# A convolution moved into PSUM by halves of 512 tokens, with three banks each for the up and down products

## The chip, the cores and the metric

The kernel runs on one core of one Trainium2 chip. The metric is the device time of one execution in microseconds (us), lower is better. The times are medians of several runs.

A core has five engines that work side by side, each through its own queue in order: TensorE (PE in the profile; PEld is its loading of weights), VectorE (DVE), ScalarE (ACT), GpSimd (POOL) and SyncE (SP, which issues the DMAs here). Tiles lie in SBUF. TensorE writes its results to PSUM, which has eight banks; a bank holds 512 float32 values in each of 128 partitions.

## The reference

Two layers of a decoder for 1024 tokens of 1024 values in float32. Each layer is a mixer (three kinds of attention) with a residual, and then the part that this change is in, a gated MLP with a causal convolution of width 3 over the tokens:

```python
h = rms_norm(x, g_ffn[l])
u = causal_dwconv(h @ w_up[l], conv_w[l], conv_b[l])   # y[t] = b + u[t]*w2 + u[t-1]*w1 + u[t-2]*w0
gate, up = u[..., :D_FF], u[..., D_FF:]                # D_FF = 2816
x = x + (jax.nn.silu(gate) * up) @ w_down[l]
```

## The kernel before

The function `ffn` computes the out-projection and the MLP of one layer. It runs once per layer: in the profiled execution the MLP's products stand from about 718 to 1450 us and from about 2140 to 2867 us.

Channels of the MLP lie on partitions and tokens along the free axis. The loop goes over the 22 blocks of 128 gate channels, each with its block of 128 up channels; the text calls one such pair of blocks a channel block. Four steps belong to each:

- **Up-projection** (`ups`, products on L958). A float32 product is made of three matmuls of operands split into a high and a low part. Two of the 22 channel blocks take eight half products per pair of blocks, the other 20 take seven by sums and differences of half blocks of weights (DVE on L990, L991, L995 and L1009, in place in the raw weights). Each half product needs two split weights `wu` (ACT copies the high part on L198, POOL subtracts it for the low part on L203) and 12 matmuls. The tag `wu` has five slots. The results are gathered in `gu` and `uu` in SBUF: by ACT (L989, L994) and, where sums are formed, by DVE from PSUM (L998, L1001, L1004, L1007, L1011).
- **Convolution** (`conv`, L1014). ACT writes `w2 * u + b` (L1016), and DVE adds the two shifted products in place with two SCALAR_TENSOR_TENSOR instructions (L1019). It is done for the gate (`yg`) and for the up part (`yu`); all of it lies in SBUF.
- **Gate** (`channels`, L1031). ACT applies Silu to `yg` in place (L1037) and DVE multiplies (L1039). All this covers 1024 tokens at once, but for the last channel block, which goes by halves of 512.
- **Down-projection** (`down7`, products on L1059). Two channel blocks together, again by seven products instead of eight: DVE and POOL form sums (L1045), ACT and POOL split (L198, L203), PE multiplies into a bank of PSUM, and DVE adds the bank to `x` (L1063). For one of the products PE goes on accumulating in a bank after DVE has read it out (`start=False` on L1089). The last two channel blocks use `down` (L1115, L1118) instead.

PSUM banks are handed out in rings by `bank(use)`. In this phase the ring `a` of the out-projection and the down products has four banks and the ring `u` of the up products has four (`B3`, L67). For the last down products `a` is set to `B4`.

The order of the instructions on each engine is settled when the program is built: a scheduler places them by its own estimate of durations, with priorities at some places, and each engine then runs its queue in that order. An instruction that has to wait holds up everything behind it on its engine.

Of the kernel before, what the change touches and what calls it, by code (L numbers as in the profile page):

```python
# [14 lines left out]
AF = mybir.ActivationFunctionType  # L15
# [3 lines left out]
S = 1024  # L19
# [9 lines left out]
# Engines of the splits into hi and lo: of the in-projection's chunks and of the rest.  # L29
# [6 lines left out]
# SBUF of each phase: runs of a start in kB and tags (name, number, kB).  # L36
# [23 lines left out]
# PSUM banks of each phase, by use.  # L60
# [6 lines left out]
B3 = {'a': (3, 6, 0, 7), 't': 'a', 'u': (4, 5, 1, 2)}  # L67
# Priorities and paces.
# [11 lines left out]
# Blocks of tokens between the down-projection and what follows it, by layer.  # L80
LAG = (2, 1)
# Channels of the up-projection that go without the seven products, and the order of these.
# [3 lines left out]
# Query heads of each chunk of the in-projection.  # L86
QH = (6, 2, 0, 0, 4, 0)
# Blocks of rows whose selection ScalarE counts.
# [8 lines left out]
class View:  # L97
    """The tiles of one phase at fixed places: each tag a ring of slots, each slot a pool of its own. Slots below cut are stacked from the left, the others from the right."""

    def __init__(self, tc, cut, top, *runs):  # L100
        """Each run is a start in kB and tags (name, number, kB) that follow one another from it."""
# [9 lines left out]
        def slot(o, side, kb):  # L111
            """A pool of one slot, which reaches kb kB, to its neighbour."""
            pool = tc.tile_pool(name=f"at{int(o * 256)}", bufs=1, side=side, reuse_waits="tile")
            self.pools[o] = self.ctx[side].enter_context(pool), int(kb * 256)
# [24 lines left out]
class Trunk:  # L139
# [19 lines left out]
    def banks(self, **uses):  # L159
        """The PSUM banks of a phase, by use."""  # L160
# [22 lines left out]
    def rstd(self, ss, n, dims):  # L183
        """(ss / dims + eps) ** -0.5 for n columns, dims per column."""
# [9 lines left out]
    def split(self, hi, lo, src, he, le):  # L194
        """src = hi + lo, each of twelve significant bits."""
# [9 lines left out]
    def rope(self, z, t, heads, width, off, half, tabs, pool, eng="vector"):  # L205
        """Rotates z[:, h, off:off + 2 * half] in place; z is [128, heads, width]."""
# [46 lines left out]
    def load_split_in(self, l, segs, pool, engines, slot):  # L253
        """The columns segs of w_in[l], split: four tiles [128, 2, 2, w], hi and lo of two rows of blocks."""
# [16 lines left out]
    def in_proj(self, hT, wc, t, after=None):  # L271
        """One token tile; its matmul M0 waits for the instruction after."""
# [18 lines left out]
    def indexer(self, zi, sc, pool, causal_diag):  # L291
        """Yields between pieces: scores of the indexer, then the selection masks, in place in sc."""
# [52 lines left out]
        # The TOPK-th largest of each row, bit by bit: the largest float that enough values reach.  # L345
        # VectorE counts the values that reach the candidate, in the upper half of the bits on values
        # cut to that half; ScalarE sums signs of differences, so that a value equal to the candidate
        # counts half, which the step after the loop repairs.
# [45 lines left out]
        # need[i]: how many of the values equal to the threshold are still to be taken.  # L394
# [35 lines left out]
    def mla_tile(self, t, ps, kpe, up, pool, outs):  # L430
        """The latents of one token tile to queries, keys and values, stored to DRAM."""
# [44 lines left out]
    def attn_prep(self, H, pool):  # L476
        """Stacked operands of one head: negated scores are the sum of the products of H["ops"]."""
# [7 lines left out]
        else:  # L485
            # [hi | lo] of keys and queries, and the keys as [lo | hi]
# [28 lines left out]
    def attn_prep_v(self, H, pool):  # L515
        """The values of one head as [hi | lo]."""
# [68 lines left out]
    def layer(self, l, hT):  # L585
        nc, tc, a = self.nc, self.tc, self.a
# [23 lines left out]
        # chunk A: indexer and the shared rotary key  # L610
# [227 lines left out]
    def ffn(self, l, mixh, xprev, xspill, hT_next):  # L838
# [96 lines left out]
        for i, j in ((1, 0), (2, 0), (1, 1), (2, 1), (4, 0), (4, 1)):  # L935
            combine(i, j)
# [267 lines left out]
```

## Time and profile before

| | |
|---|---|
| median of 3 runs | 2869.42 us (2868.08 to 2870.92) |
| profiled execution, first to last instruction (its span) | 2867.2 us |
| the median lies above that span by | 2.2 us |
| mean granted clock of TensorE | 0.988 |
| instructions in the profiled execution | 40312 |

| stretch, us | PE busy | DVE busy | ACT busy | POOL busy |
|---|---|---|---|---|
| 718 to 800 (MLP of layer 0 begins) | 71.43 | 65.81 | 33.32 | 57.22 |
| 1400 to 1450 (its end and the next norm) | 45.64 | 43.87 | 21.24 | 16.39 |
| 2140 to 2200 (MLP of layer 1 begins) | 52.02 | 46.66 | 24.65 | 35.72 |
| 2800 to 2867 (its end and the last norm) | 56.17 | 57.14 | 27.84 | 33.99 |

The page gives busy time by engine, the chain that ended last, and the costliest groups of instructions. A group is a line of the kernel, an engine, an operation and its tiles, with the number of instructions, their busy time and mean duration, and the idle time of the engine just before them with what ended it. Matmuls overlap in the pipeline, so PE's busy time is not its work: matmuls of 512 columns that follow one another start every 0.23 us, though each lasts 0.39 us. The view by stretches gives busy time in windows, the timeline gives merged instructions in order of time, and the view of waits tells who waited for whom.

### The profile page before, as it was taken

What the parts mean: (1) busy time and instruction counts of PE and PEld (TensorE: products, weight loads), DVE (VectorE), ACT (ScalarE), POOL (GpSimd) and SP (SyncE); (2) the same over time, 40 slices, a digit from 0 to 9 for tenths busy, and PEclk for the clock granted to TensorE, in tenths of its full rate; (3) what the DMA queues carried; (4) which work ended last, traced back from release to release, by engine and by line L of the source; (5) the groups of instructions that cost most, each with busy time, mean ns of one, the idle gap of its engine ahead of it and who ended that gap; (6) DMA issues with size and microseconds to landing.
All of it is one profiled execution on the core that took longest, in us unless ns stands there. A gap on an engine that the chain in (4) does not pass through costs nothing.

```text
span 2867.2 us, 40312 instructions
## 1 busy us (share of the span) xinstructions
PE 2712.0 (95%) x13576; PEld 2261.2 (79%) x13576; DVE 2353.8 (82%) x4379; ACT 1499.8 (52%) x3160; POOL 1905.0 (66%) x1910
## 2 busy tenths in 40 slices
PE   7999999999899999999999999999998999999998
PEld 7987888878677777777799878988786777777776
DVE  7679997864888888888866899978648888888888
ACT  4565758972444444444445666489624444444444
POOL 4354367961687888878634444679517888888885
PEclk9999999999999999999999999999999999999999
DMA  5322333350111111111333223233500111111112
GB/s 162 104 81 63 98 97 90 97 169 2 37 52 52 45 52 52 59 45 45 95 98 108 78 77 99 79 95 92 164 9 29 53 51 52 52 59 45 45 52 81
DMA packets 224010, 208.82 MB, mean 73 GB/s; under 512 B 21852, under 2 KB 197820, under 8 KB 223804
## 3 DMA queue, kind: packets, MB, share of 16 engines
q1 hardware_dynamic: 223804, 206.26, 23.9%
q8 instruction: 106, 1.74, 0.3%
q14 instruction: 100, 0.82, 0.1%
HBM read 153.80 MB, written 39.85 MB: 68 GB/s over the span
## 4 chain that ended last, share of the span: by engine, by line
PE 23%; POOL 21%; DVE 12%; issue 6%; ACT 3%; DMA 3%; SPq 0%; POOLq 0%; ACTq 0%; DVEq 0%
POOL wu L203 10%; PE psum L284 6%; POOL act L203 4%; POOL wd L203 4%; PE psum L924 3%; PE psum L537 3%; PE psum L958 2%; POOL wr L1045 2%; PE psum L562 2%; DMA wr<-in_w_down_dram 2%; DVE x L1063 2%; DVE yu L1019 1%; PE psum L1059 1%; DVE cut L361 1%; PE psum L1115 1%
## 5 line engine op out<-in xcount | busy, mean ns | idle before, releaser
L203 POOL TENSOR_TENSOR wu<-raw,wu 128x256 fp32r<-128x256 f32 (+1 forms) x584 | 613.2, 1069 | 176.4 <-ACT wu L198 175.2
L284 PE MATMUL psum<-wi,hT 128*128 128x384 f32 (+1 forms) x3072 | 605.7, 340 | 0.2 <-ACT hT L244 0.2
L284 PEld LDWEIGHTS psum<-wi,hT 128*128 128x128 f32 x3072 | 530.5, 190 | 9.8 <-ACT hT L244 0.6
L958 PE MATMUL psum<-hT,wu 128*128 128x512 f32 x1824 | 476.9, 396 | 41.4 <-POOL wu L203 35.9
L1059 PE MATMUL psum<-wd,act 128*128 128x512 f32 x1680 | 456.1, 396 | 15.6 <-DVE x L1063 7.7
L958 PEld LDWEIGHTS psum<-hT,wu 128*128 128x128 f32 x1824 | 341.8, 190 | 131.6 <-POOL wu L203 54.3
L198 ACT ACTIVATE wu<-raw 128x256 fp32r<-128x256 f32 (+1 forms) x584 | 228.9, 412 | 366.2 <-PE psum L958 218.2
L1063 DVE TENSOR_TENSOR x<-psum,x 128x512 f32<-128x512 f32 x640 | 411.2, 680 | 3.9 <-PE psum L1059 2.8
L958 PE MATMUL psum<-T,wu 128*128 128x512 f32 x1440 | 379.5, 399 | 33.1 <-POOL wu L203 21.5
L1059 PEld LDWEIGHTS psum<-wd,act 128*128 128x128 f32 x1680 | 312.5, 189 | 102.7 <-DVE x L1063 31.3
L958 PEld LDWEIGHTS psum<-T,wu 128*128 128x128 f32 x1440 | 267.3, 190 | 113.2 <-POOL wu L203 36.3
L547 POOL TENSOR_SCALAR pt<-pt,rl 128x128 f32<-128x128 f32 (+7 forms) x256 | 193.6, 772 | 119.1 <-DVE rl L545 103.5
L543 ACT ACTIVATE pt<-pt,nm 128x128 f32<-128x128 f32 (+7 forms) x256 | 198.9, 778 | 73.6 <-DVE nm L539 73.0
L566 DVE TENSOR_TENSOR pl<-psum,ph 128x512 fp32r<-128x512 f32 (+3 forms) x384 | 207.2, 552 | 32.8 <-ACT ph L565 28.1
L203 POOL TENSOR_TENSOR act<-yu,act 128x512 fp32r<-128x512 f32 x140 | 210.5, 1509 | 22.1 <-ACT act L198 19.3
L203 POOL TENSOR_TENSOR wd<-wr,wd 128x512 fp32r<-128x512 f32 x140 | 208.3, 1488 | 24.6 <-ACT wd L198 24.6
L191 POOL TENSOR_TENSOR rs<-ms,mhalf 128x1 f32<-128x1 f32 (+1 forms) x56 | 39.3, 701 | 252.0 <-DVE ms L188 251.9
L565 ACT ACTIVATE ph<-psum 128x512 fp32r<-128x512 f32 (+3 forms) x384 | 180.3, 488 | 35.8 <-PE psum L562 25.7
L562 PE MATMUL psum<-ident,pt 128*128 128x128 f32 x1152 | 194.2, 275 | 3.5 <-DVE QB L512 2.2
L924 PE MATMUL psum<-wo,hT 128*128 128x512 f32 x768 | 187.0, 400 | 0.0
L924 PEld LDWEIGHTS psum<-wo,hT 128*128 128x128 f32 x768 | 143.3, 189 | 31.2
L562 PEld LDWEIGHTS psum<-ident,pt 128*128 128x128 f32 x1152 | 141.4, 141 | 31.2 <-POOL pt L547 2.9
(239 smaller groups left out, 5368.1 us busy)
## 6 DMA issues: line engine op xcount, KB each, us to landing
raw<-in_w_up_dram SPq DMA_DIRECT2D x88, 512.0 KB, 3.9
raw<-in_w_in_dram SPq DMA_DIRECT2D x56, 384.0 KB, 3.3
wr<-in_w_down_dram SPq DMA_DIRECT2D x40, 512.0 KB, 3.4
z<-zst SPq DMA_DIRECT2D x96, 192.0 KB, 1.9
z<-z SPq DMA_DIRECT2D x36, 512.0 KB, 4.6
QB<-KS SPq DMA_DIRECT2D x96, 128.0 KB, 2.3
x<-in_x_dram SPq DMA_DIRECT2D x16, 512.0 KB, 4.9
raw<-in_w_o_dram SPq DMA_DIRECT2D x16, 512.0 KB, 3.8
```

Source lines behind the costliest of these rows:

```text
L198: nc.scalar.activation(hi, src, AF.Copy)
L203: (nc.vector if le == "dve" else nc.gpsimd).tensor_tensor(lo, src, r32(hi), op=ALU.subtract)
L284: mm = nc.tensor.matmul(ps[:, :w], l_, r_, start=(n == 0), stop=(n == 3 * KD - 1))
L543: nc.scalar.activation(pt, pt, AF.Exp, bias=nm, scale=-1.0, accum_out=ls[:, i % 2:i % 2 + 1])
L547: nc.gpsimd.tensor_scalar(p_, p_, rl[:, e:e + 1], 0.0, op0=ALU.mult, op1=ALU.add)
L562: nc.tensor.transpose(ps[:, (i - 4 * g) * P:(i - 4 * g + 1) * P], Pt[i][:, j * P:(j + 1) * P], self.ident)
L565: nc.scalar.activation(ph[:, off:], ps[:, off:], AF.Copy)
L566: nc.vector.tensor_tensor(pl[:, off:], ps[:, off:], r32(ph[:, off:]), op=ALU.subtract)
L924: nc.tensor.matmul(ps, l_, r_, start=(i == 0), stop=(i == 3 * KD - 1))
L958: nc.tensor.matmul(ps, l_, r_, start=(start and i == 0), stop=(stop and i == 11), skip_group_check=resume)
L1059: nc.tensor.matmul(ps, l_[:, a_, t * P:(t + 1) * P], r_[:, b_], start=(start and i == 0), stop=i == 2, skip_group_check=not start)
L1063: nc.vector.tensor_tensor(xs, ps, xs, op=ALU.add)
```

## The change

Once the out-projection is over, a new table `B5` gives three banks to `a`, three to `u`, and two to a new use `y`. The convolution is written to the `y` banks by halves of 512 tokens, for all channel blocks: ACT's first term, DVE's two in-place additions and ACT's reading for Silu are then on PSUM, and DVE's product of gate and up reads one operand from PSUM. `yg` after Silu, and the product `yu`, stay in SBUF. Transposes of the norm that follows the MLP (`t`) get four banks of their own list. Comments and docstrings are taken out too, so that line numbers move by one to three: L1016 is L1018 in the changed kernel, L1019 is L1021, L1037 is L1040, L1039 is L1042, L1059 is L1062, L1063 is L1066, L958 is L960.

```diff
-B3 = {'a': (3, 6, 0, 7), 't': 'a', 'u': (4, 5, 1, 2)}
+B3 = {'a': (3, 6, 0, 7), 't': 'a'}
+B5 = {'a': (3, 6, 0), 'u': (4, 5, 1), 'y': (2, 7), 't': (3, 6, 4, 5)}
...
             combine(i, j)
+        self.banks(**B5)
         up_src = a["w_up"][l].rearrange("(k p) n -> p k n", p=P)
...
         def conv(y, u, ch, a_, b_):
-            nc.scalar.activation(y[:, a_:b_], u[:, a_:b_], AF.Identity, bias=cw[:, 3, ch:ch + 1], scale=cw[:, 2, ch:ch + 1])
+            nc.scalar.activation(y, u[:, a_:b_], AF.Identity, bias=cw[:, 3, ch:ch + 1], scale=cw[:, 2, ch:ch + 1])
             for d in (1, 2):
                 o = max(a_, d)
-                nc.vector.scalar_tensor_tensor(y[:, o:b_], u[:, o - d:b_ - d], cw[:, 2 - d, ch:ch + 1], y[:, o:b_],
+                nc.vector.scalar_tensor_tensor(y[:, o - a_:], u[:, o - d:b_ - d], cw[:, 2 - d, ch:ch + 1], y[:, o - a_:],
                                                op0=ALU.mult, op1=ALU.add)
...
             yg, y = (pool.tile([P, S], F32, name=n, tag=tag) for n, tag in (("yg", "y"), ("yu", "Y")))
-            for a_, b_ in ((0, 512), (512, S)) if p_ == NFF - 1 else ((0, S),):
-                conv(yg, u[0], p_, a_, b_)
-                nc.scalar.activation(yg[:, a_:b_], yg[:, a_:b_], AF.Silu)
-                conv(y, u[1], NFF + p_, a_, b_)
-                nc.vector.tensor_tensor(y[:, a_:b_], yg[:, a_:b_], y[:, a_:b_], op=ALU.mult)
+            for a_, b_ in ((0, 512), (512, S)):
+                pg, pu = self.bank("y"), self.bank("y")
+                conv(pg, u[0], p_, a_, b_)
+                nc.scalar.activation(yg[:, a_:b_], pg, AF.Silu)
+                conv(pu, u[1], NFF + p_, a_, b_)
+                nc.vector.tensor_tensor(y[:, a_:b_], yg[:, a_:b_], pu, op=ALU.mult)
```

The number of instructions grows on two engines: in both layers together DVE's SCALAR_TENSOR_TENSOR go from 184 to 352 and its products of gate and up from 46 to 88, ACT's first terms from 92 to 176 and its Silu from 46 to 88. PE and POOL run as many as before. Up to the MLP of layer 0 the order on the engines stays the same. From there on the scheduler has placed all engines anew.

**On DVE**, in the middle of the loop of layer 0 (the eighth channel block that goes by seven products), the rows from the block's last but one sum `uu` on. `raw` is a block of weights before its split, `x_8525` and the like are the residual's tiles. Before:

```order
L998 TENSOR_TENSOR uu<-psum,uu 128x512
L1019 SCALAR_TENSOR_TENSOR yg<-uu,cw,yg 128x1023
L1019 SCALAR_TENSOR_TENSOR yg<-uu,cw,yg 128x1022
L991 TENSOR_TENSOR raw<-raw 128x512
L1001 TENSOR_TENSOR gu<-psum,gu 128x512
L1063 TENSOR_TENSOR x_8525<-psum,x_8525 128x512
L1063 TENSOR_TENSOR x_8597<-psum,x_8597 128x512
L1019 SCALAR_TENSOR_TENSOR yu<-gu,cw,yu 128x1023
L1019 SCALAR_TENSOR_TENSOR yu<-gu,cw,yu 128x1022
```

Of the changed kernel, the same channel block:

```order
L1021 SCALAR_TENSOR_TENSOR psum<-gu,cw,psum 128x511
L1000 TENSOR_TENSOR uu<-psum,uu 128x512
L1021 SCALAR_TENSOR_TENSOR psum<-gu,cw,psum 128x510
L1021 SCALAR_TENSOR_TENSOR psum<-uu,cw,psum 128x511
L1021 SCALAR_TENSOR_TENSOR psum<-uu,cw,psum 128x510
L993 TENSOR_TENSOR raw<-raw 128x512
L1066 TENSOR_TENSOR x_8759<-psum,x_8759 128x512
L1003 TENSOR_TENSOR gu<-psum,gu 128x512
L1042 TENSOR_TENSOR yu<-yg,psum 128x512
L1066 TENSOR_TENSOR x_8257<-psum,x_8257 128x512
L1021 SCALAR_TENSOR_TENSOR psum<-uu,cw,psum 128x512
```

The convolution's additions have become half as long, the first half of the up part goes ahead of the gate's, and the product of the first half stands before the additions of the second.

**On PE**, at the same place: `t_9159` and `T_8856` are sums of the up-projection's operand, `hT_5759` is the operand itself, `wd,act` is the down-projection. Before:

```order
L958 MATMUL psum<-t_9159,wu 128x512
L1059 MATMUL psum<-wd,act 128x512 x6
L958 MATMUL psum<-hT_5759,wu 128x512
L958 MATMUL psum<-hT_5760,wu 128x512
L958 MATMUL psum<-hT_5759,wu 128x512 x2
L958 MATMUL psum<-hT_5760,wu 128x512
L958 MATMUL psum<-hT_5759,wu 128x512
L958 MATMUL psum<-T_8856,wu 128x512
L958 MATMUL psum<-T_8858,wu 128x512
L958 MATMUL psum<-T_8856,wu 128x512 x2
```

Of the changed kernel, from the same product `t` of that channel block:

```order
L960 MATMUL psum<-t_9167,wu 128x512
L960 MATMUL psum<-t_9168,wu 128x512
L960 MATMUL psum<-t_9167,wu 128x512
L960 MATMUL psum<-hT_5759,wu 128x512 x2
L960 MATMUL psum<-hT_5760,wu 128x512
L1062 MATMUL psum<-wd,act 128x512 x4
L960 MATMUL psum<-hT_5759,wu 128x512
L960 MATMUL psum<-T_8856,wu 128x512
L960 MATMUL psum<-T_8858,wu 128x512
L960 MATMUL psum<-hT_5759,wu 128x512
L960 MATMUL psum<-hT_5760,wu 128x512
```

Before, the up-projection's matmuls stand together behind the six of the down-projection: 6 of `hT`, 24 of `T` and 12 of `hT` with none of the down-projection between them. In the changed kernel the products are mixed with one another and with the down-projection in smaller groups.

## The prediction

> **What bounds the kernel now.** The first view is the page's table of engines, and then the busy time in two stretches of 600 us from the middle of each layer's MLP, the only part that the change touches. The columns are the stretch, its length, and the busy time of PE, PEld, DVE, ACT and POOL with the number of instructions, then PE's clock and the DMA share.
>
> ```profile
> PE 2712.0 (95%) x13576; PEld 2261.2 (79%) x13576; DVE 2353.8 (82%) x4379; ACT 1499.8 (52%) x3160; POOL 1905.0 (66%) x1910
> 800.00:1400.00 600.00, 566.02 (x2392) 443.83 (x2391) 518.37 (x629) 261.40 (x497) 499.59 (x416) 0.99 0.16 49
> 2200.00:2800.00 600.00, 564.34 (x2377) 441.81 (x2377) 516.26 (x620) 258.09 (x493) 496.12 (x415) 0.99 0.16 50
> ```
>
> PE is the fullest engine, but its busy time flatters it, since matmuls overlap. What PE needs for its work is read from a run without a wait:
>
> ```profile
> 1034.89 1.20 PE L958 MATMUL psum<-hT,wu 128*128 128x512 f32 x4 [1.44 <-POOL wu L203]
> 1036.22 5.73 PE L958 MATMUL psum<-T,wu 128*128 128x512 f32 x24
> 1041.79 2.88 PE L958 MATMUL psum<-hT,wu 128*128 128x512 f32 x12
> ```
>
> Twelve matmuls take 2.88 us, of which the last one's own length is about 0.39 us, so one starts every (2.88 - 0.39) / 11 = 0.226 us. The 2392 matmuls of the first stretch need 2392 x 0.226 = 541 us, those of the second 537 us: PE loses 59 and 63 us there, 122 us in all. A channel block has 7 x 12 = 84 matmuls of the up-projection and 42 of the down-projection, so a stretch holds 2392 / 126 = 19.0 blocks: a block takes 31.6 us, PE needs 28.5 us of it, DVE 27.3 us, POOL 26.3 us and ACT 13.8 us. Three engines are nearly full, each in a fixed order, so short waits decide.
>
> The next view is that of the waits on PE over the whole span, and for the weight loader in windows around each MLP (700 to 1440 and from 2120 us on): who waits on whom, the sum in us, the number, the longest.
>
> ```profile
> PE psum L958 <- POOL wu L203: 57.4, 51, 3.1
> PE psum L958 <- ACT wu L198: 12.3, 8, 2.7
> PE psum L1059 <- DVE x L1063: 7.7, 22, 1.2
> PEld psum L958 <- POOL wu L203: 44.1, 44, 3.1
> PEld psum L958 <- POOL wu L203: 46.4, 45, 3.5
> ```
>
> The largest wait is for POOL's low part of the up weights: 57.4 us as idle time of PE, and 44.1 + 46.4 = 90.5 us as idle time of the loader, which sees a stall earlier because PE still drains its pipeline. The true loss lies between the two.
>
> **Why POOL is late.** POOL's subtraction of one size has very different lengths, and so have VectorE's steps of the convolution. The lines of the groups, with count, busy time and mean ns:
>
> ```profile
> L203 POOL TENSOR_TENSOR wu<-raw,wu x584: 713/752/2286, 626.9 to 2830.6; 128x256 fp32r<-128x256 f32 x193, 128x512 fp32r<-128x512 f32 x2
> L203 POOL TENSOR_TENSOR wu<-raw,wu 128x256 fp32r<-128x256 f32 (+1 forms) x584 | 613.2, 1069 | 176.4 <-ACT wu L198 175.2
> 1018.78 1.42 POOL L203 TENSOR_TENSOR wu<-raw,wu 128x256 fp32r<-128x256 f32 x2
> 1017.22 3.67 DVE L1063 TENSOR_TENSOR x<-psum,x 128x512 f32<-128x512 f32 x6
> 1031.65 3.19 POOL L203 TENSOR_TENSOR wu<-raw,wu 128x256 fp32r<-128x256 f32 x2 [2.25 <-ACT wu L198]
> 1031.30 2.96 DVE L1019 SCALAR_TENSOR_TENSOR yg<-uu,cw,yg 128x1023 f32<-128x1023 f32 x2 [1.31 <-ACT yg L1016]
> ```
>
> The subtraction takes 713 ns at best (minimum, median and maximum stand first) and 1069 ns in the mean. Beside six DVE additions that read one operand from PSUM, two of them take 1.42 us; beside two steps of the convolution, which read both operands from SBUF, two take 3.19 us, and PE then waits 1.44 us at 1034.89. The convolution suffers as well. So DVE with two operands in SBUF and POOL hinder each other, and DVE with one in PSUM hinders nobody.
>
> **The change, part by part.** First DVE.
>
> ```profile
> L1019 DVE SCALAR_TENSOR_TENSOR yg<-gu,cw,yg 128x1023 f32<-128x1023 f32 (+1 forms) x44 | 81.2, 1844 | 23.7 <-ACT yg L1016 23.7
> L1019 DVE SCALAR_TENSOR_TENSOR yu<-uu,cw,yu 128x1023 f32<-128x1023 f32 (+1 forms) x44 | 79.2, 1801 | 0.1
> L1019 DVE SCALAR_TENSOR_TENSOR yg<-uu,cw,yg 128x1023 f32<-128x1023 f32 (+4 forms) x48 | 69.0, 1443 | 27.1 <-ACT yg L1016 26.4
> L1019 DVE SCALAR_TENSOR_TENSOR yu<-gu,cw,yu 128x1023 f32<-128x1023 f32 (+4 forms) x48 | 67.2, 1401 | 7.2 <-ACT yu L1016 6.3
> L1039 DVE TENSOR_TENSOR yu<-yg,yu 128x1024 f32<-128x1024 f32 (+1 forms) x46 | 58.1, 1263 | 1.3 <-ACT yg L1037 1.1
> L1063 DVE TENSOR_TENSOR x<-psum,x 128x512 f32<-128x512 f32 x640 | 411.2, 680 | 3.9 <-PE psum L1059 2.8
> L995 DVE TENSOR_TENSOR raw<-raw 128x512 f32<-128x512 f32 x40 | 27.7, 692 | 54.1 <-POOL wu L203 54.1
> L1019 DVE SCALAR_TENSOR_TENSOR yg<-uu,cw,yg 128x512 f32<-128x512 f32 x2 | 1.5, 742 | 0.0
> L1019 DVE SCALAR_TENSOR_TENSOR yg<-gu,cw,yg x44: 1269/1857/2412, 756.0 to 2803.2; 128x1023 f32<-128x1023 f32 x22, 128x1022 f32<-128x1022 f32 x22
> ```
>
> Now 81.2 + 79.2 + 69.0 + 67.2 = 296.6 us of convolution and 58.1 us of products: 354.7 / 44 = 8.06 us for each of the 44 channel blocks. Afterwards there are 8 half steps and 2 half products. A half product has one operand in PSUM, like the 680 ns row. A step that reads and writes one PSUM bank is in no row. From below it is bounded by that 680 ns; from above by 1.27 us: a full step takes 1269 ns at best, 0.53 us more than the 742 ns of a half one in SBUF, and a bank that had to be gone to twice for each element would cost a half step that much again. I take 742 ns, the row of the same operation and size: 8 x 0.742 + 2 x 0.68 = 7.30 us, 0.76 us less for each block, 33 us less on DVE in all. None of it counts in the sum: it lies beside PE's products, and only makes room.
>
> [...]
>
> Second, **POOL**. The other DVE operations with two operands in SBUF stay:
>
> ```profile
> L1045 DVE TENSOR_TENSOR yu<-yu 128x512 f32<-128x512 f32 x80 | 92.6, 1177 | 0.1
> L1045 DVE TENSOR_TENSOR wr<-wr 128x512 f32<-128x512 f32 x40 | 47.4, 1185 | 26.4 <-POOL wd L203 26.2
> L1009 DVE TENSOR_TENSOR raw<-raw 128x512 f32<-128x512 f32 x40 | 51.0, 1276 | 0.0
> L991 DVE TENSOR_TENSOR raw<-raw 128x512 f32<-128x512 f32 x40 | 38.1, 951 | 9.9 <-POOL wu L203 9.9
> L990 DVE TENSOR_TENSOR raw<-raw 128x512 f32<-128x512 f32 x40 | 33.3, 834 | 8.5 <-DMA raw<-in_w_up_dram 7.6 <-POOL wu L203 0.4
> ```
>
> With L995 they make 290.1 us, so the convolution and its product are 354.7 of 644.8 us, 55% of the time in which the two engines can meet. The 584 subtractions take 584 x (1.069 - 0.713) = 208 us more than at their best; 55% of that, 114 us or 2.6 us for each block, goes. Of the 57.4 to 90.5 us that PE loses to POOL, the same share is 32 to 50 us. I take 50 us: the loader's figure is nearer to the loss at a stall, and at 1034.89 the hindered pair was late by 1.77 us, more than PE's whole wait. The ends are 32 us and, if all such stalls go, 90.5 us.
>
> Third, **ACT**. Its first term and Silu by full and half lengths (the half ones are the last channel block's in layer 0):
>
> ```profile
> L1016 ACT ACTIVATE yu<-uu,cw 128x1024 f32<-128x1024 f32 x22 | 27.4, 1246 | 48.0 <-DVE uu L1001 40.8 <-POOL wu L203 4.5 <-POOL T L203 2.6
> L1016 ACT ACTIVATE yg<-uu,cw 128x512 f32<-128x512 f32 x2 | 1.6, 808 | 2.2 <-DVE uu L998 2.2
> L1037 ACT ACTIVATE yg<-yg 128x1024 f32<-128x1024 f32 x42 | 44.5, 1060 | 65.7 <-DVE yg L1019 65.6
> L1037 ACT ACTIVATE yg<-yg 128x512 f32<-128x512 f32 x2 | 1.3, 634 | 2.1 <-DVE yg L1019 2.1
> ```
>
> A block has 2 x 1.246 + 1.060 = 3.55 us of them now and 4 x 0.808 + 2 x 0.634 = 4.50 us then. PSUM as ACT's target is in no row; I take SBUF's, with the half Silu's 0.634 us and the full first term's 1.246 us as ends. ACT is busy 13.8 of 31.6 us for a block, so I count nothing; without that room it would cost 0.95 us a block, 42 us. The new handovers between ACT and DVE (a half must be read by Silu, or multiplied, before its bank takes the next half) hold up what is queued behind them: on ACT the high parts of `wu`, on DVE the additions of L1063, for which PE waits.
>
> Fourth, the **banks**. A wait for L1063 costs PE 7.7 / 22 = 0.35 us now, at most 1.2 us. I counted in the program's order how many matmuls lie between the last use of a bank and the down-projection's next one in it. Where a new product starts, 18 of 320 places have 12 or fewer before and 26 after; where PE goes on in a bank that DVE has just read, 2 of 240 and 40. Twelve matmuls are 2.7 us, enough for an addition that is not itself held up. I charge all 46 new short places 0.35 us, 16 us; the ends are nothing and 46 x 1.2 = 55 us. For the up-projection such places go from 20 to 2, so its third bank costs nothing.
>
> The **sum**: 2867.2 - 50 + 16 = 2833 us of span, and with the 2.2 us between span and median **2835 us**. PE alone would allow 122 us, so this asks for 28% of its loss.
>
> **The rivals.** *The relief stays on POOL.*
>
> ```profile
> L198 ACT ACTIVATE wu<-raw 128x256 fp32r<-128x256 f32 (+1 forms) x584 | 228.9, 412 | 366.2 <-PE psum L958 218.2 <-DVE raw L1009 91.4 <-DVE raw L995 12.8
> ```
>
> For: POOL idles 175.2 us ahead of `wu` for ACT, and ACT in its turn 91.4 us for DVE's last sum of weights; with the hindrance gone the stall may end as late on that chain, while the banks cost their 16 us. Against: the stall above ended on POOL's 3.19 us. Time: half of the low end, 16 us, less the banks' 16 us, so 2869 us (2860 to 2876).
>
> *DVE becomes the bound (slower).* Its place is the in-place step in a bank. It decides from (8.06 - 1.36) / 8 = 0.84 us for a half step. If one takes 0.95 us, half of the slower rows' 1.9 us, a block has 8.96 us instead of 8.06; at DVE's present filling of 27.3 / 31.6 = 86% that lengthens it by 1.0 us, 46 us in all: 2915 us. [...] Against: the 680 ns and 742 ns rows.
>
> *The banks cost more than POOL gains (slower).* In-order DVE puts an addition behind a held convolution. It decides from 50 / 46 = 1.1 us for each new short place. At 1.2 us, with the low end of POOL's gain: 2869 - 32 + 55 = 2892 us. Against: half steps let DVE reach L1063 after 0.7 us, not 1.8 us.
>
> **How the numbers follow.** Forecast 0.62 (its own range 2800 to 2853, POOL's low end with the banks' 16 us), relief on POOL 0.16, DVE the bound 0.10, banks 0.12. A measurement tells about 0.2%, 6 us, from no change. Faster: 0.62 and a third of the second case, 0.67. Same: half of the second and a little of the fourth, 0.11. Slower: the rest, 0.22. The range leaves out 2892 and 2915 us, with their 0.22 less a part that lands lower: 2800 (50 us of POOL's gain raised to nearly 70, no cost of banks) to 2878 us.
>
> **What would show it.** Right: L1021's half steps at 0.68 to 0.78 us with hardly any spread; `wu` on POOL at a mean of some 0.87 us (1.069 less 114 / 584); PE's wait for POOL under 30 us; its wait for L1066 of 15 to 25 us. Wrong: half steps above 0.84 us; POOL's mean down and PE's waits now for ACT's `wu` or DVE's sums; or waits for L1066 above 50 us.

## The result, and the profile after

| | before | changed |
|---|---|---|
| median, us | 2870.17 (2868.08 to 2874.37, 4 runs) | 2797.03 (2793.93 to 2802.98, 4 runs) |
| ratio to before | | 0.9747, interval 0.9734 to 0.976 |
| span of the profiled execution, us | 2867.2 | 2791.9 |
| mean granted clock of TensorE | 0.988 | 0.989 |

The kernel is faster by 73 us; forecast were 34 us. The time lies 3 us below the range's low end of 2800 us.

First the page's table of engines, of the changed kernel:

```profile
PE 2680.4 (96%) x13576; PEld 2264.6 (81%) x13576; DVE 2305.0 (83%) x4589; ACT 1527.2 (55%) x3286; POOL 1729.4 (62%) x1910
```

DVE is busy 48.8 us less with 210 instructions more, POOL 175.6 us less with the same number. The busy time in a stretch of 580 us of each MLP:

```profile
800.00:1380.00 580.00, 562.42 (x2421) 454.52 (x2420) 509.28 (x735) 277.46 (x559) 425.32 (x420) 0.99 0.18 54
2165.00:2745.00 580.00, 562.39 (x2430) 455.40 (x2430) 502.65 (x726) 276.90 (x561) 424.30 (x424) 0.99 0.17 52
```

At 0.226 us the matmuls need 547 and 549 us, so PE loses 33 + 31 = 64 us where it lost 122, for slightly more work. A channel block takes 580 / (2421 / 126) = 30.2 us, not 31.6. Next the groups of instructions that the change was to make shorter (count, busy time, mean ns, idle time before), and one line's durations as minimum, median and maximum:

```profile
L1021 DVE SCALAR_TENSOR_TENSOR psum<-gu,cw,psum 128x512 f32<-128x512 f32 (+2 forms) x176 | 131.9, 750 | 23.6 <-ACT psum L1018 22.0
L1021 DVE SCALAR_TENSOR_TENSOR psum<-uu,cw,psum 128x512 f32<-128x512 f32 (+2 forms) x176 | 131.5, 747 | 14.7 <-ACT psum L1018 13.8
L1042 DVE TENSOR_TENSOR yu<-yg,psum 128x512 f32<-128x512 f32 x88 | 59.6, 677 | 21.5 <-POOL act L204 19.9 <-ACT yg L1040 1.1
L204 POOL TENSOR_TENSOR wu<-raw,wu 128x256 fp32r<-128x256 f32 x584 | 481.6, 842 | 301.9 <-ACT wu L199 295.8 <-DVE x L1066 3.7 <-DVE raw L992 1.2
L1018 ACT ACTIVATE psum<-uu,cw 128x512 f32<-128x512 f32 x88 | 68.6, 779 | 48.8 <-DVE uu L1013 22.9 <-DVE uu L1000 14.5 <-DVE yu L1042 10.4
L1040 ACT ACTIVATE yg<-psum 128x512 f32<-128x512 f32 x88 | 51.9, 590 | 58.0 <-DVE psum L1021 58.0
```

```profile
L1021 DVE SCALAR_TENSOR_TENSOR psum<-uu,cw,psum x176: 736/746/757, 733.2 to 2751.4; 128x512 f32<-128x512 f32 x88, 128x511 f32<-128x511 f32 x44, 128x510 f32<-128x510 f32 x44
```

All 176 of these half steps take 736 to 757 ns, where a full one of `yg` from `gu` took 1269 to 2412. Convolution and products are 131.9 + 131.5 + 59.6 = 323.0 us instead of 354.7. POOL's subtraction is at a mean of 842 ns, not 1069. The timeline of POOL and DVE in the middle of layer 0's MLP shows why:

```profile
1012.70 1.54 DVE L1021 SCALAR_TENSOR_TENSOR psum<-uu,cw,psum 128x511 f32<-128x511 f32 x2 [0.19 <-ACT psum L1018]
1013.47 0.74 POOL L204 TENSOR_TENSOR wu<-raw,wu 128x256 fp32r<-128x256 f32 x1 [0.87 <-ACT wu L199]
1017.88 1.43 POOL L204 TENSOR_TENSOR wu<-raw,wu 128x256 fp32r<-128x256 f32 x2
1018.52 0.74 DVE L1021 SCALAR_TENSOR_TENSOR psum<-gu,cw,psum 128x512 f32<-128x512 f32 x1
```

Beside the convolution a subtraction now takes 0.72 to 0.74 us; before, two took 3.19 us.

The waits on PE over the span (sum in us, number, longest), and the loader's in the windows around the two MLPs (700 to 1440 and 2120 to 2870 us):

```profile
PE psum L960 <- ACT wu L199: 19.4, 6, 5.6
PE psum L1062 <- DVE x L1066: 12.3, 14, 2.9
...
PE psum L960 <- POOL wu L204: 9.6, 6, 2.7
...
PEld psum L960 <- POOL wu L204: 6.6, 6, 3.4
PEld psum L960 <- POOL wu L204: 8.0, 6, 3.4
```

PE's wait for POOL is 9.6 us instead of 57.4, and the loader's 6.6 + 8.0 = 14.6 us instead of 90.5. The wait for the additions to `x` grew by 4.6 us, that for ACT's `wu` by 7.1 us. No single wait of the MLP stands out any more; the largest is now the one for ACT's `wu`.

### The profile page after: what moved, and what is told of

It is laid out like the page before. It is cut to its first block, busy times and chain, and to the rows that moved or that the text cites. A ratio compares the mean times of both kernels' runs of the same rounds, so it can differ in the third digit from the quotient of the medians.

```text
span 2791.9 us, 40705 instructions
## 1 busy us (share of the span) xinstructions
PE 2680.4 (96%) x13576; PEld 2264.6 (81%) x13576; DVE 2305.0 (83%) x4589; ACT 1527.2 (55%) x3286; POOL 1729.4 (62%) x1910
## 4 chain that ended last, share of the span: by engine, by line
PE 66%; DVE 18%; POOL 7%; issue 4%; DMA 3%; ACT 2%; POOLq 0%; ACTq 0%; SPq 0%; DVEq 0%
PE psum L960 19%; PE psum L285 12%; PE psum L1062 9%; PE psum L925 6%; PE psum L538 6%; PE psum L563 4%; DVE cut L362 2%; DVE x L1066 2%; DVE psum L1021 2%; PE psum L574 2%; PE psum L573 2%; POOL wu L204 2%; PE psum L571 1%; PE psum L1118 1%; POOL wd L204 1%
## 5 line engine op out<-in xcount | busy, mean ns | idle before, releaser
L204 POOL TENSOR_TENSOR wu<-raw,wu 128x256 fp32r<-128x256 f32 x584 | 481.6, 842 | 301.9 <-ACT wu L199 295.8
L960 PE MATMUL psum<-hT,wu 128*128 128x512 f32 x1824 | 483.1, 397 | 21.1 <-ACT wu L199 11.2
L1062 PE MATMUL psum<-wd,act 128*128 128x512 f32 x1680 | 468.1, 395 | 21.1 <-DVE x L1066 12.3
L199 ACT ACTIVATE wu<-raw 128x256 fp32r<-128x256 f32 x584 | 231.3, 415 | 431.1 <-PE psum L960 293.2
L1066 DVE TENSOR_TENSOR x<-psum,x 128x512 f32<-128x512 f32 x640 | 418.0, 680 | 30.9 <-PE psum L1062 29.7
L960 PEld LDWEIGHTS psum<-hT,wu 128*128 128x128 f32 x1824 | 348.3, 192 | 99.4 <-ACT wu L199 12.9
L1062 PEld LDWEIGHTS psum<-wd,act 128*128 128x128 f32 x1680 | 314.3, 189 | 103.1 <-DVE x L1066 24.3
L960 PE MATMUL psum<-T,wu 128*128 128x512 f32 x1440 | 375.4, 391 | 11.0 <-ACT wu L199 8.2
L960 PEld LDWEIGHTS psum<-T,wu 128*128 128x128 f32 x1440 | 269.3, 188 | 73.2 <-ACT wu L199 10.4
L204 POOL TENSOR_TENSOR act<-yu,act 128x512 fp32r<-128x512 f32 x140 | 195.2, 1394 | 42.2 <-ACT act L199 41.3
L204 POOL TENSOR_TENSOR wd<-wr,wd 128x512 fp32r<-128x512 f32 x140 | 200.2, 1430 | 11.6 <-ACT wd L199 11.2
```

The source lines that it names most:

```text
L199: nc.scalar.activation(hi, src, AF.Copy)
L204: (nc.vector if le == "dve" else nc.gpsimd).tensor_tensor(lo, src, r32(hi), op=ALU.subtract)
L960: nc.tensor.matmul(ps, l_, r_, start=(start and i == 0), stop=(stop and i == 11), skip_group_check=resume)
L1062: nc.tensor.matmul(ps, l_[:, a_, t * P:(t + 1) * P], r_[:, b_], start=(start and i == 0), stop=i == 2, skip_group_check=not start)
L1066: nc.vector.tensor_tensor(xs, ps, xs, op=ALU.add)
```

## The experiments

All ratios are to the kernel before on the same chip. "Against the changed kernel" is the difference of the two ratios times 2867 us, good to some 6 us.

### Halves, banks and place apart

The change does three things: halves of 512 tokens, three banks instead of four, and the place in PSUM. Three kernels do them apart.

```diff
# e1, of the changed kernel: halves and three banks, all in SBUF
-                pg, pu = self.bank("y"), self.bank("y")
+                pg, pu = yg[:, a_:b_], y[:, a_:b_]
# e2, of the kernel before: three banks only
-B3 = {'a': (3, 6, 0, 7), 't': 'a', 'u': (4, 5, 1, 2)}
+B3 = {'a': (3, 6, 0, 7), 't': 'a'}
+B5 = {'a': (3, 6, 0), 'u': (4, 5, 1), 't': (3, 6, 4, 5)}
# e3, of the kernel before: halves only
-            for a_, b_ in ((0, 512), (512, S)) if p_ == NFF - 1 else ((0, S),):
+            for a_, b_ in ((0, 512), (512, S)):
```

(e2 also switches to its `B5` after the out-projection, as the change does.)

> The changed kernel with the convolution back in SBUF: still halves of 512 tokens, still three banks each for the up and down products (the two y banks lie idle), and an order on PE that is as mixed as the changed kernel's (2 runs of 30 or more up matmuls in a row, against 22 before). Theory A (the gain is that DVE and POOL no longer hinder each other): it falls back to 2855 to 2880 us, POOL's wu at a mean of about 1.05 us, PE's wait for POOL's wu at 40 us or more. Theory B (the gain is the order: short steps and products that are mixed more finely): 2795 to 2815 us.

> The kernel before with three banks each for the up and down products and nothing else. Its order on PE is mixed too (4 runs of 30 or more up matmuls in a row). Theory A with the prediction's charge for banks: 2870 to 2890 us. Theory B: 2800 to 2840 us, since the finer mixing alone lets POOL keep up.

> The kernel before with the convolution by halves of 512 tokens for all channel blocks, in SBUF, with four banks each as before. Theory A: about 2870 us or a little more (half steps cost 2 x 742 - 1269 = 0.2 us more for each full one). Theory B, if it is the halves: 2800 to 2840 us.

Measured: e1 2952.20 us, ratio 1.0304 (1.0289 to 1.032); e2 2913.53 us, 1.0176 (1.0157 to 1.0195); e3 2900.36 us, 1.0118 (1.0101 to 1.0135). Each is slower than before: halves by 34 us, banks by 50 us, both by 87 us. The place in PSUM, the only difference between e1 and the changed kernel's program, is worth 160 us with what the scheduler makes of it. None of the three times lies in a range that was expected: theory A had the direction, but e1 is 72 and e2 24 us above its upper end, and e3 is 30 us above its 2870. The waits on PE of e1, and then of e3, where line numbers are those of before:

```profile
PE psum L1062 <- DVE x L1066: 86.9, 64, 4.0
PE psum L960 <- ACT wu L199: 20.1, 10, 5.1
...
PE psum L960 <- POOL wu L204: 9.1, 12, 2.4
```

```profile
PE psum L1059 <- DVE x L1063: 54.9, 40, 3.9
PE psum L958 <- ACT wu L198: 33.3, 30, 5.1
...
PE psum L958 <- POOL wu L203: 6.2, 10, 1.5
```

And the group of POOL's subtraction in e3:

```profile
L203 POOL TENSOR_TENSOR wu<-raw,wu 128x256 fp32r<-128x256 f32 (+1 forms) x584 | 554.2, 967 | 226.1 <-ACT wu L198 212.9 <-POOL wu L203 6.4 <-issue 3.8
```

In e3 the subtraction is still hindered (967 ns in the mean, where the changed kernel has 842), and yet PE's wait for it is 6.2 us: most of the hindrance stayed, the wait went, and the time went to DVE, whose additions come late. So the size of PE's wait for POOL said little of what relieving POOL would be worth, though e3's other order has a part in this that no run separates.

In e2 the banks' loss shows at another place, the up products' banks:

```profile
PE psum L960 <- ACT uu L991: 45.5, 18, 4.5
```

PE waits 45.5 us there until ACT has copied an up product out of its bank, and 18.4 us for the additions to `x`, against 7.7 before. In e1 the wait on ACT's L991 is 19.9 us. The changed kernel has three banks for the up products too, and there the loader's waits for it are 1.1 us in each layer.

### One half of the convolution in SBUF

```diff
# e4: the gate's in SBUF                      # e5: the up part's in SBUF
-                pg, pu = self.bank("y"), self.bank("y")
+                pg, pu = yg[:, a_:b_], self.bank("y")        # e4
+                pg, pu = self.bank("y"), y[:, a_:b_]         # e5
```

> The changed kernel with the gate's convolution in SBUF and the up part's in PSUM, both by halves; the product keeps one operand in PSUM. Half of the additions are of the hindered kind again, no product. The run with the up part in SBUF gave 2896 us and had the products too. Both theories: between the changed kernel's 2797 us and 2896 us, about 2855 us if the time goes with the hindered DVE steps.

> The changed kernel with the gate's convolution in PSUM and the up part's in SBUF, both by halves; the product of gate and up then has both operands in SBUF again. Of 355 us of DVE steps that left the hindered kind, about 207 us come back. Theory A: in between, about 2797 + 73 x 207 / 355 = 2840 us (2825 to 2855). Theory B: 2795 to 2815 us.

Measured: e4 2847.61 us, 0.9931 (0.9915 to 0.9947); e5 2896.14 us, 1.011 (1.0093 to 1.0126). Against the changed kernel that is 53 and 104 us. In e5 the product of gate and up has both operands in SBUF again too. e4 is near the 2855 us that were expected, e5 is 41 us above the upper end of theory A. The two do not separate the engines, since the scheduler made another order for each. The order had to be held.

### The gate in SBUF, in the changed kernel's order

In e11 the program is that of e4, but every engine's queue is held to the sequence of the changed kernel by dependencies between neighbours that carry no semaphore.

> The changed kernel with the gate's convolution in SBUF, every engine's queue held to the changed kernel's order, instruction for instruction. The only difference left is that 176 of 352 half steps have both operands in SBUF. If the place alone makes the time: 2840 to 2860 us, like the same kernel in its own order (2848 us). If the order was what PSUM brought: 2797 to 2810 us.

Measured: 2871.39 us, 1.0013 (0.9999 to 1.0027), 76 us against the changed kernel, all that it had gained, and more than either expectation had. In its own order the same program (e4) gave back 53 us. The groups of its convolution:

```profile
L1021 DVE SCALAR_TENSOR_TENSOR yg<-uu,cw,yg 128x511 f32<-128x511 f32 (+1 forms) x88 | 101.1, 1149 | 5.9 <-ACT yg L1018 5.4
L1021 DVE SCALAR_TENSOR_TENSOR yg<-gu,cw,yg 128x511 f32<-128x511 f32 (+1 forms) x88 | 99.1, 1126 | 15.6 <-ACT yg L1018 13.9
L1021 DVE SCALAR_TENSOR_TENSOR psum<-gu,cw,psum 128x511 f32<-128x511 f32 (+1 forms) x88 | 65.7, 746 | 8.0 <-ACT psum L1018 7.8
L1021 DVE SCALAR_TENSOR_TENSOR psum<-uu,cw,psum 128x511 f32<-128x511 f32 (+1 forms) x88 | 65.7, 746 | 5.2 <-ACT psum L1018 5.0
```

The same half steps take 1126 to 1149 ns in the mean in SBUF and 746 ns in a bank. The shortest half steps are alike, 737 and 739 ns in SBUF (the kernel before), 735 and 736 in a bank (the changed kernel): what is longer in SBUF is longer by hindrance. DVE's convolution is 331.6 us instead of 263.4, so 68 us longer (all of DVE is busy 69 us longer), and POOL is busy 1784.7 us, 55 us longer. Both engines are late at once; the next kernels make them late one by one.

### DVE late, POOL late, both late, in the same order

The queues are held to the changed kernel's order, with short instructions added: on DVE multiplications of 220 columns of a bank by 1.0, on POOL a subtraction of 16 columns. They do not lengthen the other engine: POOL is busy 9 us less in e14, DVE 9 us less in e15.

```diff
# e14: one on DVE behind each convolution; e18: two behind the gate's, none behind the up part's
                 conv(pg, u[0], p_, a_, b_)
+                nc.vector.tensor_scalar(pg[:, :220], pg[:, :220], 1.0, None, op0=ALU.mult)
                 conv(pu, u[1], NFF + p_, a_, b_)
+                nc.vector.tensor_scalar(pu[:, :220], pu[:, :220], 1.0, None, op0=ALU.mult)
# e15: behind five of eight pairs of subtractions of wu; e16 = e14 and e15, e19 = e18 and e15
+                nc.gpsimd.tensor_tensor(w[1][:, 1, 0, :16], src[:, 256:272], r32(w[1][:, 0, 0, :16]), op=ALU.subtract)
```

> The changed kernel with every engine's queue held to its own order, and behind each convolution's two additions in a bank one more VectorE instruction, a multiplication of 220 columns of that bank by 1.0: 176 of them, about 0.39 us each, some 68 us, as much as VectorE was longer in the kernel with the gate's halves in SBUF in this order (2871 us). It adds nothing to GpSimd and doesn't hinder it. If that kernel's 74 us came through VectorE's lateness, 2850 to 2871 us, with PE's wait for the additions to x at 35 to 50 us. If they came through GpSimd's lateness, 2797 to 2815 us. If the two share it evenly, about 2830 us.

> The changed kernel with every queue held to its own order, and behind five of eight pairs of GpSimd's subtractions of the up weights one more subtraction of 16 columns: 180 of them, 0.31 us each, some 56 us of GpSimd, as much as GpSimd was longer in the kernel with the gate's halves in SBUF in this order. VectorE gets nothing. If that kernel's 74 us came through GpSimd's lateness, 2850 to 2871 us, with PE's wait for the low parts of the up weights at 25 us or more. If they came through VectorE's, 2797 to 2815 us.

> Both additions of work at once, 68 us of VectorE and 56 us of GpSimd, in the changed kernel's order. If lengthening of the two engines in a fixed order is all that the kernel with the gate's halves in SBUF suffers from, 2860 to 2882 us, near its 2871 us. If there is something else (the clock, contention of the weight loads, a spread of durations), it stays below 2850 us.

> The changed kernel in its own order again, with the same 176 multiplications of 220 columns (0.395 us each, 69.6 us of VectorE), now two of them behind each of the gate's convolutions and none behind the up part's, which is where the kernel with the gate's halves in SBUF was longer. If only the total counts, 2817 us as with one behind each convolution. If the place counts, since the gate's sum goes on through ScalarE's Silu before the product can be formed and two in a row double the lateness of what stands behind, 2825 to 2850 us.

> As before, and GpSimd's 180 subtractions of 16 columns (52 us) as well. If place and both lengthenings are what the kernel with the gate's halves in SBUF suffers from, 2855 to 2875 us, near its 2871 us. If only the totals count, 2833 us as with one multiplication behind each convolution; then some 35 us of that kernel's loss come from something that these additions do not imitate, such as the two engines being late at the same moments.

| kernel | added | busy longer, DVE and POOL, us | time, us | ratio | against the changed kernel |
|---|---|---|---|---|---|
| e14 | DVE 69.6 us, spread | 45.6, -9.1 | 2816.86 | 0.9828 (0.9813 to 0.9843) | 23 us |
| e15 | POOL 52.3 us | -9.2, 51.5 | 2808.17 | 0.9799 (0.9782 to 0.9815) | 15 us |
| e16 | both | 47.4, 47.1 | 2833.49 | 0.9888 (0.9873 to 0.9903) | 40 us |
| e18 | DVE 69.5 us, all at the gate | 58.3, -15.3 | 2849.82 | 0.9939 (0.9921 to 0.9958) | 55 us |
| e19 | e18's and POOL 52 us | 54.5, 39.0 | 2861.26 | 0.9978 (0.9965 to 0.999) | 66 us |

DVE's busy time grew by less than was added, since other steps of it became shorter. Spread evenly, neither engine gives back e11's 76 us: e14 and e15 are both low, and e16, below 2850 us, says that something besides the two sums counts, though DVE's busy time grew less in it than in e11. The place counts. Put where e11 has its lengthening, the same 69.5 us of DVE cost 55 us, 32 us more than when spread, and with POOL's 66 of the 76 us, within what was expected if place and lengthening are all. So DVE's lateness carries most of it, and POOL's adds 11 to 17 us.

Two things stay open. In e18 the multiplications stand at the gate and also two in a row; no run has two in a row behind the up part, so it isn't shown which of the two makes them dear. And no run holds the changed kernel's order with nothing added: what the holding itself costs lies in all five times, 15 us at most by e15. The differences among the five are free of it: the 69.6 us of DVE cost 25 us spread (e16 against e15) and 51 us at the gate (e19 against e15).

How DVE's lateness turns into a stall of PE is to be seen in e18 in three views: the timeline, then the same place of the changed kernel, then windows of 10 us of e18 (busy time of PE, PEld, DVE, ACT, POOL, then the granted clock). L1014 is the last sum of weights, L1011 in the changed kernel.

```profile
1027.72 0.83 DVE L1044 TENSOR_SCALAR psum<-psum 128x220 f32<-128x220 f32 x2
1037.44 1.15 DVE L1014 TENSOR_TENSOR raw<-raw 128x512 f32<-128x512 f32 x1
1038.62 0.72 ACT L202 ACTIVATE wu<-raw 128x256 fp32r<-128x256 f32 x2 [3.40 <-DVE raw L1014]
1039.09 1.22 PE L963 MATMUL psum<-T,wu 128*128 128x512 f32 x2 [3.11 <-ACT wu L202]
1040.11 1.91 PE L1067 MATMUL psum<-wd,act 128*128 128x512 f32 x4
1041.82 1.05 PE L963 MATMUL psum<-hT,wu 128*128 128x512 f32 x2
```

```profile
1029.01 0.68 DVE L1011 TENSOR_TENSOR raw<-raw 128x512 f32<-128x512 f32 x1
1029.72 0.73 ACT L199 ACTIVATE wu<-raw 128x256 fp32r<-128x256 f32 x2 [0.40 <-DVE raw L1011]
1030.22 0.70 PE L960 MATMUL psum<-T,wu 128*128 128x512 f32 x2
```

```profile
1030.00:1040.00 10.00, 6.89 (x29) 5.43 (x28) 10.00 (x15) 4.49 (x11) 9.74 (x8) 0.91 0.01 4
1040.00:1050.00 10.00, 10.00 (x35) 7.93 (x35) 6.38 (x9) 1.76 (x4) 3.73 (x5) 0.75 0.33 98
```

DVE is full for 10 of 10 us and so reaches L1014 late. The 0.83 us shown are a part of that; sums that took longer beside POOL, as L1014 itself with 1.15 us for 0.68, are another. ACT stands idle for it for 3.40 us, where the changed kernel has 0.40, and PE for ACT for 3.11 us, where the changed kernel has no idle time. Then the four matmuls at 1040.11 start (1041.82 - 1040.11) / 4 = 0.43 us apart, not 0.226; the granted clock of that window is 0.75. PE's table of that kernel says the same in sum:

```profile
PE psum L1067 <- DVE x L1071: 34.5, 30, 2.9
PE psum L963 <- ACT wu L202: 32.2, 10, 6.5
```

These waits are 22 and 13 us longer than in the changed kernel. The rest is the clock (the last column but two), first of the changed kernel, then of e18:

```profile
720.00:1400.00 680.00, 654.12 (x2824) 529.63 (x2822) 590.33 (x825) 320.90 (x636) 484.36 (x463) 0.98 0.19 56
2150.00:2800.00 650.00, 610.32 (x2633) 492.67 (x2631) 552.78 (x799) 298.74 (x600) 443.92 (x444) 0.99 0.17 54
```

```profile
720.00:1400.00 680.00, 636.53 (x2695) 513.31 (x2694) 596.93 (x873) 310.82 (x617) 465.55 (x454) 0.97 0.16 50
2150.00:2800.00 650.00, 607.46 (x2568) 489.39 (x2567) 569.76 (x842) 295.50 (x593) 453.32 (x445) 0.97 0.16 48
```

From these clocks I estimate that the lower clock costs about 680 x 0.01 + 650 x 0.02 = 20 us more, and 22 + 13 + 20 makes up the 55 us. The pages agree: PE is idle 38.0 us longer than in the changed kernel and busy 19.8 us longer for the same 13576 matmuls.

### More work on one engine, planned and not

```diff
# e7: DVE, 512 columns, 176 times, planned by the scheduler; e10_narrow: the same with 8 columns
                 conv(pg, u[0], p_, a_, b_)
+                nc.vector.tensor_scalar(pg, pg, 1.0, None, op0=ALU.mult)
                 conv(pu, u[1], NFF + p_, a_, b_)
+                nc.vector.tensor_scalar(pu, pu, 1.0, None, op0=ALU.mult)
# e8: POOL, 288 subtractions of 16 columns, planned
+            nc.gpsimd.tensor_tensor(w[0][:, 1, 0, :16], src[:, :16], r32(w[0][:, 0, 0, :16]), op=ALU.subtract)
```

In e10_unplanned the instructions are those of e7, but in the order that the scheduler made for e10_narrow.

> The changed kernel with one more VectorE instruction for each half of each convolution: a multiplication by 1.0 of the bank in place, 176 in all, at about 0.65 us some 115 us of DVE work that touches no SBUF operand and so does not hinder POOL. In the halves-in-SBUF run hindrance made DVE's convolution and products 175 us longer and POOL's splits some 110 us. Theory D (PE waits for a late DVE): 2860 to 2910 us, with PE's wait for the additions to x back at 50 us or more. Theory P (the prediction's: PE waits for a late POOL): 2795 to 2820 us.

> The changed kernel with a small extra subtraction on POOL for every second split of up weights (16 columns done again): 292 more instructions, at about 0.3 us some 90 us of POOL work, each in front of a product; DVE is left alone. Theory D: 2795 to 2815 us. Theory P: 2850 us or more, with PE's wait for POOL back above 40 us.

> The base of the next run: the changed kernel with the 176 extra multiplications by 1.0 on 8 columns of the bank only, some 0.15 us each, 25 us of DVE work that the scheduler knows of. At the rate of the run with 121 us of them (43 us for 121 us): 2806 us, 2795 to 2820 us.

> The 176 multiplications by 1.0 on 512 columns, 121 us of DVE work that hinders nobody, in the order of the run with 8 columns: the order doesn't know how long they are, as it doesn't know of hindrance. If lateness against the plan is what makes hindrance dear: well above the 2840 us of the same instructions in an order made for them, 2870 to 2910 us. If only the amount of DVE work counts: 2835 to 2850 us.

Measured: e7 (121 us on DVE, 688 ns each) 2840.36 us, 0.9921 (0.9891 to 0.9952); e8 (88.5 us on POOL, 313 ns each) 2812.29 us, 0.9807 (0.9791 to 0.9822); e10_narrow (29.6 us) 2828.31 us, 0.9862 (0.9837 to 0.9887); e10_unplanned 2870.33 us, 1.0014 (0.9999 to 1.0028). POOL's 88.5 us cost 17 us, DVE's 121 us cost 50 us when planned and 77 us when not: the same instructions, 27 us apart in two orders. POOL's subtraction takes 847 ns in the mean in e7, 842 in the changed kernel. e7 lies between the two theories, with a wait for the additions of 19.8 us where theory D had 50; e8 is as theory D had it. That a lengthening is dearer when the order knows nothing of it is not shown by this: e10_narrow's 29.6 us cost 33 us, where 9 were expected, so the order that e10_unplanned takes over is already a poor one, and against it 91 us more of DVE cost 44 us, 0.48 of a us each, near e7's 50 / 121 = 0.41. What in that order costs so much stays open.

### Further on

```diff
# e9: one of DVE's two sums of down weights to POOL; e17 = e9 and e13
-CW = ('gpsimd', 'vector', 'vector', 'gpsimd')
+CW = ('gpsimd', 'gpsimd', 'vector', 'gpsimd')
# e13: four banks for the down products, one for the convolution
-B5 = {'a': (3, 6, 0), 'u': (4, 5, 1), 'y': (2, 7), 't': (3, 6, 4, 5)}
+B5 = {'a': (3, 6, 0, 7), 'u': (4, 5, 1), 'y': (2,), 't': (3, 6, 4, 5)}
```

> The changed kernel with one of the sums of down weights (20 of 60 on DVE, some 1.05 us each) moved from DVE to POOL, where one takes about 1.4 us. Theory D: 10 to 20 us faster than the changed kernel, 2777 to 2790 us, since DVE gets 21 us back. Theory P: the same or slower, 2795 to 2815 us.

> The changed kernel with four banks for the down products and one for the convolution, which gate and up part then share. If the down products' banks still cost the changed kernel what the banks-only run showed (49 us for the two banks taken away): 10 to 25 us faster, less what the single y bank costs. If they cost little once DVE is on time (its wait for the additions is 12.3 us): the same or slower, 2797 to 2830 us.

> The changed kernel with four banks for the down products, three for the up products and one for the convolution, and one of the two sums of the down weights that VectorE forms given to GpSimd. If the gains of the two edits (9 us and 6 us, each measured alone against the changed kernel) add, 2782 us. If GpSimd, lengthened by that sum, takes the place of VectorE, 2788 us or more.

Measured: e9 2791.39 us, 0.9739 (0.9723 to 0.9755); e13 2788.04 us, 0.9718 (0.9692 to 0.9744); e17 2806.29 us, 0.9787 (0.9768 to 0.9807). e13 has the lowest ratio of all, but its interval meets the changed kernel's, and e9 can't be told from the changed kernel. Together, in e17, they cost 11 us against the changed kernel instead of gaining more, on the side of the expectation that had GpSimd as the next limit; which of its waits that comes from was not settled. What e13 says of the banks: a fourth bank for the down products, paid for with one of the convolution's two, brought 8 us net; by the intervals it is worth something between nothing and 16 us. What the convolution's bank costs by itself is not separated.

## Why the prediction was right in its direction and wrong in its size

**Half steps: right.** Forecast 742 ns, measured 747 and 750, with hardly any spread; product 677 for 680 ns. The shortest half steps differ by 1 to 4 ns between SBUF (before) and a bank (changed), and in the mean of e11 the bank is the faster one, 746 ns against 1126 to 1149. The rival of DVE as the bound fell with the half steps.

**POOL: right in the mechanism, too small in the sum.** The mean is 842 ns, forecast 870; the group's busy time fell by 613.2 - 481.6 = 131.6 us, forecast 114. The term in the sum was 50 us, 55% of the loader's 90.5 us; that wait fell by 76 us. The share of DVE's time was thus not a measure of the wait, and e3 lost most of the wait with POOL still slow: it was the place where the lateness of several engines ended, not POOL's own account.

**DVE's saving: the step that failed.** The prediction had it at 33 us and said: "None of it counts in the sum: it lies beside PE's products, and only makes room." The saving is 31.7 us; the zero was wrong. DVE forms the weights that ACT copies for PE and empties the banks that PE needs, in one fixed queue, so a late gate makes all of these late. The loader's waits for DVE itself show a part of it, before and then changed, in the window of layer 0's MLP:

```profile
PEld psum L1059 <- DVE x L1063: 15.5, 28, 1.7
PEld psum L958 <- DVE gu L1001: 6.0, 9, 1.5
PEld psum L1115 <- DVE gu L1001: 4.2, 1, 4.2
...
PEld psum L1062 <- DVE x L1066: 12.4, 15, 3.3
```

The wait for `gu` is gone, and that for `x` is shorter with a bank less. In both windows together the loader's waits that ended on DVE fell from 49.3 to 27.6 us. What ended on POOL or ACT because DVE was late is not in this.

The held kernels give a price for it. A us by which DVE is busy longer cost 25 / 56.6 = 0.44 us spread (e16 against e15) and up to 55 / 58.3 = 0.94 us at the gate (e18). DVE's busy time fell by 48.8 us in all; at these two prices that is 21 to 46 us, which were missing. For POOL the runs give 11 / 54.3 = 0.20 (e19 against e18) to 17 / 56.2 = 0.30 us (e16 against e14); its 175.6 us less are 35 to 53 us, so the 50 us charged there lie near the upper end of what POOL's own work brought. Both sums are estimates: the prices were measured at the changed kernel, in its order, and carried to the way from before to it.

**Banks: over-charged.** Forecast 16 us; PE's wait for the additions grew by 4.6 us, to 12.3 us where 15 to 25 were the sign, and the loader's fell from 31.2 to 24.4 us. In SBUF the same three banks cost 50 us (e2), and there PE waited 45.5 us for the up products' banks, whose third bank the prediction had at nothing. The rival "banks cost more" had its mechanism in e1, where PE waits 86.9 us for the additions; in the changed kernel DVE comes on time.

**ACT: nearly right to count nothing.** First terms take 779 ns and Silu 590, and PE's wait for ACT's `wu` grew by 7.1 us. The rival that the stall would end as late on ACT and the sums ahead of it fell with this.

So the sum was off at three terms: POOL's wait (50 forecast, 76 measured), the banks (16 and 5), and DVE's saving, set at nothing. The first two close the gap in arithmetic, since 2867.2 - 76 + 5 + 2.2 = 2798 us; but the 76 us may contain what DVE's being on time took off the wait for POOL, as e3 suggests. With POOL's 35 to 53, DVE's 21 to 46 and the banks' 5 the estimate is 51 to 94 us faster, which holds the measured 73 but is too wide to prove the division. How much of the gain is DVE's, how much POOL's, and how much the scheduler's new order brought by itself stays open: the old order can't be held, since the instructions are others.

## What to carry to other kernels

Where several engines are nearly full and each runs a fixed queue, a saving on an engine that isn't the bound is not worth zero (here a us of DVE was worth 0.44 us in e16 and up to 0.94 us in e18): price it by how late that engine makes the work behind it, and add work at one place at a time to see where lateness is dear (23 us in e14, 55 us in e18). A wait in the table shows where lateness ended, not who owns it: another change may move it to a different engine (in e3 the wait for POOL was 6.2 us, with POOL's subtraction still at 967 ns, and that for DVE 54.9 us), and relieving its named cause may take off more than its share (here 76 us of the loader's 90.5, forecast 50). The same program was 23 us slower when held to another kernel's order (e11 against e4), so hold the order before comparing engines, and run the held order with nothing added too.

## What the runs showed of the hardware

- A half step in place in a PSUM bank, its shifted operand in SBUF, takes 735 to 757 ns in all 352 cases of the changed kernel, with POOL busy 62% of the time; the same in SBUF takes 1126 to 1149 ns in the mean beside POOL (e11); before, it took 737 ns at its shortest and 742 ns in the mean of two. Reading and writing one bank costs nothing extra here.
- One stall of PE in e18 was paid for twice. The rows that follow on those shown above, after 3.11 us of idle time, are:

```profile
1042.67 1.91 PE L1067 MATMUL psum<-wd,act 128*128 128x512 f32 x4
1044.38 1.84 PE L963 MATMUL psum<-T,wu 128*128 128x512 f32 x6
1046.06 0.86 PE L1067 MATMUL psum<-wd,act 128*128 128x512 f32 x3
```

From 1039.09 to 1044.38 us 12 matmuls start 0.44 us apart, about half the rate of 0.226, and only within the row at 1044.38 PE comes back to speed. To 1046.06 us 18 matmuls start in 6.97 us, where 18 x 0.226 = 4.07 us would do: 2.9 us more, nearly as much as the stall. So here the half rate follows 3.11 us of idle time and lasts at least 5.29 us; the granted clock is 0.75 from 1040 to 1050 us and 1.00 in the ten us after that. The profiled executions in which PE waits longer for the additions to `x` have the lower mean clock: 86.9 us and 0.973 in e1, 41.6 us and 0.978 in e19, 12.3 us and 0.989 in the changed kernel.
